# Three output-gate blocks of a hyena, attention and expert layer are computed between the first blocks of the hyena's projection instead of beside the attention

## The chip, the cores and the metric

One core of a Trainium2 chip runs the whole program. The metric is the device time of one execution in microseconds (us). The kernel before was run three times: 1930.4, 1916.2 and 1919.15 us, median 1919.15 us.

## What is computed

The reference is one transformer-like layer for 512 tokens of width 1024. The part that matters here is the token mixer:

```
z = h @ w_in + b_in
q, k, v = z[..., COL_Q:COL_K], z[..., COL_K:COL_V], z[..., COL_V:COL_G_HY]
y_hy = hyena(z[..., COL_HY:COL_Q]) @ w_hy_out
y_na = attend(q, k, v) @ w_na_out
gate = sigmoid(z[..., COL_G_HY:N_PROJ])
merged = gate[..., :D_MODEL] * y_hy + gate[..., D_MODEL:] * y_na
return merged @ w_out
```

`z` has 40 column blocks of 128: 12 for the hyena (blocks 0 to 3 are its value, 4 to 11 its two gates), 12 for the attention's q, k and v, and 16 for the output gates (blocks 24 to 39). The hyena convolves with long filters by Fourier transforms; the attention works on a window of the token grid and on 256 context tokens. A layer of sparse experts follows and takes the larger part of the time; the change does not touch it.

## The kernel before, in words

TensorE (PE) does all products, with 32-bit floats that are split into a high and a low half: a weight block is fetched into a tile `raw`, ScalarE (ACT) rounds it to `wh` (line 206), VectorE (DVE) subtracts to get `wl` (line 207). `raw` has three buffers, `wh` and `wl` two each, and all the stages share them. A column block of `z` is one call of `z_col` (line 469): `weights` fetches and splits, `project` (line 229) issues 16 matmuls of 512 columns with `wh` (line 235) and 8 with `wl` (line 237), and the sum stands in one of the two PSUM tiles called `a`. ACT then drains that tile with the bias added: into `zpad` for a hyena block (line 489 in `hy_block`), into `gz` or `t` for an output gate (line 591 in `gate`). `gate` stores its block to DRAM (line 592, queue SP); the merge at the end of the mixer loads all 16 again (`gl`, line 924).

The stages around the change, in the order of time:

- Filters and the hyena's first blocks (`run`, lines 850 to 862). The loop over `cb` computes blocks 0 to 3 of `z` and, after each, one step of the second filter (`drain(f1, 1)`). Behind block 1 it loads the context, computes its norm (`rstd`: sums of squares, transposes on line 405, a reduction on 407, a square root on 408, a reciprocal on 409, transposes back on 412) and its modulated form `hc`.
- The hyena (`hyena`, line 543): transposes of `y` (505), spectra (`spectrum`, 225 to 227 into tiles `s`, sums on DVE in 330 to 334), products with the filters (513 to 523), inverse transforms, and the eight gate blocks of the hyena. Beside it the modulation vector 2 is built from eight blocks of `w_ada` (`late_module`: ACT in 447 and 451, GpSimd additions in 452), and six output gates are computed at the steps in `HG`, the first of them at step 1.
- The attention (lines 876 to 909): 16 units, four blocks of queries for each of four pairs of heads. Step n issues the scores of unit n (`attn_scores`), the transposes of unit n-1 (`attn_turn`), one step of the projection for the next pair of heads, then `GATES[n]` items of the list `fill`, then the product with v of unit n-2 (`attn_out`, 749 and 750) and the store of unit n-3 (759). `fill` holds what is left of the output gates, then the eight blocks of the hyena's output product (`hy_out`, 12 matmuls each). What is left after step 16 is issued at step 17, with `issue_after(turn)`.
- The merge (`gated`, `out_proj`).

The order written here is not the final one: a scheduler in the compiler moves instructions on each engine by its own estimate, within what the data allow. Each engine then works through its own list in that order.

Of the kernel before, what the change touches and what calls it, by code (L numbers as in the profile page):

```python
# [153 lines left out]

GATES = [2, 1, 0, 1, 0, 1, 0, 1, 1, 1, 0, 1, 2, 2, 1, 2, 1]

LA = (0, 2)

# [11 lines left out]
class Kernel:  # L172
# [613 lines left out]
    def run(self, st):  # L786
# [17 lines left out]
        def drain(g, n=None):  # L804
            while n is None or n > 0:
                try:
                    next(g)
                except StopIteration:
                    return False
                n = None if n is None else n - 1  # L810
            return True

        dst = ExitStack()
        with ExitStack() as s1:
            dft = self.t(self.pool(dst, "dft", side="right"), "dft", [128, 2, 2, 4, 256], F32R)
            fp = self.pool(s1, "filt", side="right")
            cst = ExitStack()
            with ExitStack() as s0:
                xp = self.pool(s0, "x", side="left")
                cc = self.load(k, "cc")  # L820
                self.silu = k.tile([128, 8, 2], F32, name="silu_c")
                nc.scalar.activation(self.silu, cc, AF.Silu)
                mlp = self.filter_mlp(fp)
                cond = self.conditioning(xp)
                drain(mlp, 1)
                xT = self.load(xp, "xT")
                steps = [next(cond) for _ in range(2)]
                self.ident = self.load(k, "ident")
                for n, t in (("bada", "b_ada"), ("ng", "norm_g"), ("bin", "b_in"), ("cw", "cw"), ("skip", "skip")):
                    setattr(self, n, self.load(k, t))  # L830
                drain(mlp, 1)
                steps += [next(cond) for _ in range(2)]
                drain(mlp)
                r = self.rstd(xp, xT, 4)
                with self.tc.issue_after(self.squared):
                    nc.gpsimd.dma_start(dft, self.A["dft"])
                steps += [next(cond) for _ in range(2)]
                f0 = self.filters(0, fp, dft, steps[F4AT])
                drain(f0, 1)
                steps += list(cond)  # L840
                self.hold = steps[-1]
                self.modulate(xp, self.h, xT, self.a1[:, :, 0], self.sh1[:, :, 0], r)
            hst2 = ExitStack()
            vp = self.pool(hst2, "hyv", side="left")
            y = [self.t(vp, "yv", [128, 512], bufs=4) for _ in range(4)]
            cp = self.pool(cst, "hctx", side="left")
            self.hc = [self.t(cp, f"hc{x}", [128, 8, 256], F32R) for x in range(2)]
            zst = ExitStack()
            zp = self.pool(zst, "hyz", side="left")
            f1 = self.filters(1, fp, dft, self.hold)  # L850
            drain(f0)
            drain(f1, 1)
            for cb in range(4):
                self.hy_block(cb, y[cb], zp)
                if cb == 1:
                    xc = self.load(zp, "ctxT")
                    rc = self.rstd(zp, xc, 2)
                    self.modulate(zp, self.hc, xc, self.a1[:, :, 1], self.sh1[:, :, 1], rc, bufs=4)
                drain(f1, 1)
            pending = list(range(16))  # L860
            drain(f1)
            zst.close()
        yst = ExitStack()
# [12 lines left out]
        with ExitStack() as s1:  # L876
# [13 lines left out]
            for n in range(len(units) + 3):  # L890
# [12 lines left out]
                with self.tc.issue_after(turn) if n >= 17 else ExitStack():  # L903
                    for _ in range(min(GATES[n], len(fill)) if n < 17 else len(fill)):
                        fill.pop(0)()
# [398 lines left out]
```

## Time and profile before

| | |
|---|---|
| median of three runs | 1919.15 us |
| the profiled execution | 1923.32 us, span 1921.6 us, granted PE clock 0.98 |
| PE busy | 1817.9 us (95%) |
| DVE busy | 1507.1 us (78%) |
| ACT busy | 851.1 us (44%) |
| GpSimd busy | 583.1 us (30%) |

Times in the views below are us from the start of the span. A group's row gives a line, an engine, an operation, the tiles written and read, and how many. A row of the timeline gives start, duration, engine, line and, in brackets, the idle time of the engine ahead of it with what ended it. A row by stretch gives for each engine its busy time with the number of instructions, the granted PE clock as a share of 2.4 GHz, the share of the DMA engines and GB/s.

### The profile page before, as it was taken

What the parts mean: (1) busy time and instruction counts of PE and PEld (TensorE: products, weight loads), DVE (VectorE), ACT (ScalarE), POOL (GpSimd) and SP (SyncE); (2) the same over time, 40 slices, a digit from 0 to 9 for tenths busy, and PEclk for the clock granted to TensorE, in tenths of its full rate; (3) what the DMA queues carried; (4) which work ended last, traced back from release to release, by engine and by line L of the source; (5) the groups of instructions that cost most, each with busy time, mean ns of one, the idle gap of its engine ahead of it and who ended that gap; (6) DMA issues with size and microseconds to landing.
All of it is one profiled execution on the core that took longest, in us unless ns stands there. A gap on an engine that the chain in (4) does not pass through costs nothing.

```text
span 1921.6 us, 26565 instructions
## 1 busy us (share of the span) xinstructions
PE 1817.9 (95%) x9747; PEld 1566.6 (82%) x9747; DVE 1507.1 (78%) x2755; ACT 851.1 (44%) x1271; POOL 583.1 (30%) x363
## 2 busy tenths in 40 slices
PE   6999999999999988889999999999999999999987
PEld 1577887888877777789988898899999999987875
DVE  7869874556578699998997867887777777778876
ACT  2554334555563533336876333333333333333342
POOL 3443000000002533331221444444444444433431
PEclk9989999999999999999999999999999999999999
DMA  8445323322277322236988988989998888778874
GB/s 302 139 145 174 121 91 97 94 85 79 79 267 243 99 75 72 76 129 237 329 311 308 352 300 306 334 312 323 328 324 297 317 317 308 279 272 305 296 264 130
DMA packets 166843, 428.29 MB, mean 223 GB/s; under 512 B 14679, under 2 KB 70167, under 8 KB 162744
## 3 DMA queue, kind: packets, MB, share of 16 engines
q1 hardware_dynamic: 129128, 288.16, 44.5%
q0 software_dynamic: 37584, 138.43, 19.4%
q8 instruction: 76, 1.25, 0.3%
q14 instruction: 55, 0.45, 0.1%
HBM read 386.69 MB, written 37.75 MB: 221 GB/s over the span
## 4 chain that ended last, share of the span: by engine, by line
PE 62%; DVE 18%; issue 6%; DMA 5%; POOL 3%; ACT 2%; SPq 0%; ACTq 0%; DVEq 0%; POOLq 0%
PE a L235 24%; PE a L237 11%; PE s L225 5%; PE s L226 5%; PE s L227 5%; POOL row L1272 3%; PE t L225 2%; PE t L227 2%; PE t L226 2%; DVE f L1193 2%; PE s L1258 1%; PE s L1259 1%; DMA row<-in_u_rows,ei 1%; DVE vl L207 1%; DVE h2n L1286 1%
## 5 line engine op out<-in xcount | busy, mean ns | idle before, releaser
L235 PE MATMUL a<-h,wh 128*128 128x384 f32 (+1 forms) x2944 | 617.2, 359 | 9.8 <-ACT ring L1015 5.2
L235 PEld LDWEIGHTS a<-h,wh 128*128 128x128 f32 x2944 | 528.1, 191 | 58.2 <-ACT ring L1015 5.5
L206 ACT ACTIVATE wh<-raw 128x1024 fp32r<-128x1024 f32 (+1 forms) x208 | 213.6, 1027 | 370.5 <-DMA raw<-in_u_cols 156.3
L237 PE MATMUL a<-h,wl 128*128 128x384 f32 (+1 forms) x1472 | 317.0, 354 | 0.0
L1272 POOL DMA_INDIRECT row<-in_u_rows,ei x128 | 184.7, 1443 | 335.4 <-DVE row L1277 319.6
L1272 POOL DMA_INDIRECT row<-in_v_rows,ei x128 | 198.2, 1549 | 272.5 <-DVE h2n L1286 259.1
L237 PEld LDWEIGHTS a<-h,wl 128*128 128x128 f32 x1472 | 262.8, 189 | 17.6
L207 DVE TENSOR_TENSOR wl<-raw,wh 128x1024 fp32r<-128x1024 f32 (+1 forms) x173 | 202.9, 1173 | 52.2 <-ACT wh L206 30.8
L226 PE MATMUL s<-vl,wsh 128*128 128x512 f32 x512 | 201.3, 393 | 9.8 <-DVE vl L207 9.8
L227 PE MATMUL s<-vh,wsl 128*128 128x512 f32 x512 | 198.8, 390 | 0.0
L1277 DVE SCALAR_TENSOR_TENSOR row<-row,h2n 128x1024 f32<-128x1024 f32 x128 | 155.2, 1221 | 51.4 <-DMA row<-in_u_rows,ei 51.2
L206 ACT ACTIVATE wsh<-w 128x384 fp32r<-128x384 f32 x128 | 66.9, 523 | 277.5 <-PE t L226 145.8
L225 PE MATMUL s<-vh,wsh 128*128 128x512 f32 x512 | 176.4, 391 | 3.7 <-ACT vh L206 2.2
L1286 DVE SCALAR_TENSOR_TENSOR h2n<-row,dots,h2n 128x1024 f32<-128x1024 f32 x127 | 162.5, 1280 | 17.9 <-DMA row<-in_v_rows,ei 17.7
L397 POOL TENSOR_TENSOR sqs<-sqs,sq 128x512 f32<-128x512 f32 (+1 forms) x20 | 31.5, 1576 | 430.7 <-ACT sq L396 430.0
L207 DVE TENSOR_TENSOR vl<-raw,vh 128x1024 fp32r<-128x1024 f32 x128 | 155.9, 1218 | 7.7 <-ACT vh L206 7.7
L207 DVE TENSOR_TENSOR wsl<-w,wsh 128x384 fp32r<-128x384 f32 x128 | 78.1, 610 | 97.4 <-ACT wsh L206 97.3
L206 ACT ACTIVATE vh<-raw 128x1024 fp32r<-128x1024 f32 x128 | 134.4, 1050 | 22.1 <-DMA raw<-in_v_rows 21.6
L207 POOL TENSOR_TENSOR wl<-raw,wh 128x1024 fp32r<-128x1024 f32 x35 | 87.0, 2486 | 129.1 <-PE a L237 116.3
L226 PEld LDWEIGHTS s<-vl,wsh 128*128 128x128 f32 x512 | 96.3, 188 | 31.0 <-DVE vl L207 13.8
L225 PEld LDWEIGHTS s<-vh,wsh 128*128 128x128 f32 x512 | 95.9, 188 | 22.6 <-ACT vh L206 3.9
L227 PEld LDWEIGHTS s<-vh,wsl 128*128 128x128 f32 x512 | 96.4, 188 | 20.0 <-issue 0.2
(357 smaller groups left out, 3030.6 us busy)
## 6 DMA issues: line engine op xcount, KB each, us to landing
raw<-in_u_cols SPq DMA_DIRECT2D x128, 512.0 KB, 4.2
raw<-in_v_rows SPq DMA_DIRECT2D x128, 512.0 KB, 4.2
Gd<-st SPq DMA_DIRECT2D x24, 1024.0 KB, 5.2
G<-Gd SPq DMA_DIRECT2D x16, 1536.0 KB, 11.1
raw<-in_w_in SPq DMA_DIRECT2D x40, 512.0 KB, 3.5
adaw<-in_w_ada SPq DMA_DIRECT2D x16, 512.0 KB, 4.6
raw<-in_w_q SPq DMA_DIRECT2D x16, 512.0 KB, 3.4
wada<-in_w_ada SPq DMA_DIRECT2D x8, 512.0 KB, 8.9
```

What stands on the lines that cost most here:

```text
L206: return (nc.scalar.activation(hi, src, AF.Copy).ins, (nc.vector if eng == "v" else nc.gpsimd).tensor_tensor(lo, src, hi, ALU.subtract).ins)
L207: (nc.vector if eng == "v" else nc.gpsimd).tensor_tensor(lo, src, hi, ALU.subtract).ins)
L225: t.matmul(out, a[0], b[0], start=start, stop=False)
L226: t.matmul(out, a[0], b[1], start=False, stop=False)
L227: return t.matmul(out, a[1], b[0], start=False, stop=stop).ins
L235: t.matmul(out, w[0][:, c, :], h[x][:, c, :], start=(c == 0 and x == 0), stop=False)
L237: i = t.matmul(out, w[1][:, c, :], h[0][:, c, :], start=False, stop=(c == n - 1))
L397: self.squared = (nc.vector if db in dve else nc.gpsimd).tensor_tensor(acc, acc, sq, ALU.add).ins
L1193: V.tensor_tensor(m, mv[:, :, 0, :], mv[:, :, 1, :], ALU.add)
L1272: nc.gpsimd.indirect_dma_start(out=r, out_offset=None, in_=self.A[tab], in_offset=bass.IndirectOffsetOnAxis(ap=ei[:, n:n + 1], axis=0))
L1277: V.scalar_tensor_tensor(r, r, 1.0, h2n, op0=ALU.mult, op1=ALU.mult, accum_out=dots[:, n:n + 1])
L1286: V.scalar_tensor_tensor(acc, r, dots[:, n:n + 1], acc, op0=ALU.mult, op1=ALU.add)
```

## The change

The list of pending gates is made ahead of the loop over the hyena's first blocks, and after blocks 1, 2 and 3 one gate is computed (output gates 0, 1 and 2), with its `gz` in the pool of that stage. Thirteen gates remain: six beside the hyena as before, and seven in `fill` where there were ten. `GATES` has 15 items now where it had 17, so that with the list of 15 nothing is left over for step 17.

```
-GATES = [2, 1, 0, 1, 0, 1, 0, 1, 1, 1, 0, 1, 2, 2, 1, 2, 1]
+GATES = [1, 1, 0, 1, 0, 1, 0, 1, 1, 0, 1, 1, 1, 2, 1, 2, 1]
...
             drain(f0)
             drain(f1, 1)
+            pending = list(range(16))
             for cb in range(4):
                 self.hy_block(cb, y[cb], zp)
...
                 drain(f1, 1)
-            pending = list(range(16))
+                if cb:
+                    self.gate(pending.pop(0), zp)
             drain(f1)
```

The list of PE behind the context's norm, before: `a_874` and `a_946` are the hyena's blocks 2 and 3, `a_1103` is the output gate of step 1 of the hyena, `s_1039` its first spectrum. Each block has 16 rows of line 235 and one of line 237.

```order
L412 MATMUL a_805<-ident_144,rs_801 128x128 x2
L235 MATMUL a_874<-h_80,wh_870 128x512
...
L237 MATMUL a_874<-h_80,wl_871 128x512 x8
...
L237 MATMUL a_946<-h_80,wl_943 128x512 x8
...
L237 MATMUL a_1103<-h_80,wl_1100 128x512 x8
L225 MATMUL s_1039<-yth_1010,dft_85 128x256
```

The same place after the change: `a_874` is output gate 0, `a_908` the hyena's block 2, `a_980` gate 1, `a_1014` block 3, `a_1070` gate 2, `a_1205` the gate of step 1.

```order
L412 MATMUL a_805<-ident_144,rs_801 128x128 x2
L235 MATMUL a_874<-h_80,wh_870 128x512
...
L237 MATMUL a_874<-h_80,wl_871 128x512 x8
...
L237 MATMUL a_908<-h_80,wl_905 128x512 x8
...
L237 MATMUL a_980<-h_80,wl_977 128x512 x8
...
L237 MATMUL a_1014<-h_80,wl_1011 128x512 x8
...
L237 MATMUL a_1070<-h_80,wl_1067 128x512 x8
...
L237 MATMUL a_1205<-h_80,wl_1202 128x512 x8
L225 MATMUL s_1141<-yth_1112,dft_85 128x256
```

All three added blocks stand in one row of six, behind the transposes of the context's norm (line 412) and ahead of the hyena's first spectrum.

ACT beside these blocks, before: it drains block 2 (`zpad_899`), block 3 (`zpad_971`) and the gate (`gz_1128`); `raw_1186` is a block of `w_ada`.

```order
L489 ACTIVATE zpad_899<-a_874,b_in_150 128x4x8x16
L206 ACTIVATE hc_107_446<-md_835 128x256
L431 ACTIVATE md_845<-md_845,mod_368,a_393 128x256
L206 ACTIVATE hc_107_446<-md_845 128x256
L206 ACTIVATE hc_107_446<-md_840 128x256
L451 ACTIVATE raw_1186<-raw_1186,silu_c 128x1024
L489 ACTIVATE zpad_971<-a_946,b_in_150 128x4x8x16
L206 ACTIVATE yth_1010<-t_1007 128x256
L206 ACTIVATE yth_1017<-t_1014 128x256
L447 ACTIVATE adaacc_1003<-raw_1035,silu_c 128x1024
L591 ACTIVATE gz_1128<-a_1103,b_in_150 128x512
```

After the change, from the drain of block 2 to the first `yth`: `wh_1201` is the high half of the weights for the sixth block, `raw_1195` and `raw_1288` are blocks of `w_ada`.

```order
L489 ACTIVATE zpad_933<-a_908,b_in_150 128x4x8x16
L206 ACTIVATE wh_1066<-raw_1064 128x1024
L451 ACTIVATE raw_1195<-raw_1195,silu_c 128x1024
L591 ACTIVATE gz_1005<-a_980,b_in_150 128x512
L206 ACTIVATE wh_1201<-raw_1199 128x1024
L489 ACTIVATE zpad_1039<-a_1014,b_in_150 128x4x8x16
L451 ACTIVATE raw_1288<-raw_1288,silu_c 128x1024
L591 ACTIVATE gz_1095<-a_1070,b_in_150 128x512
L206 ACTIVATE yth_1112<-t_1109 128x256
L206 ACTIVATE yth_1119<-t_1116 128x256
```

The drains of three blocks now stand right behind instructions that read a freshly fetched tile `raw`.

The list of PE at the end of the attention, before: the last transposes (line 733) of unit 15, a block of `hy_out` (`a_5259`), then the product with v of unit 15.

```order
L750 MATMUL a_5231<-vv_4031,pcl_5101 128x64
L733 MATMUL t_5197<-ident_144,s_5079 128x128 x2
L733 MATMUL t_5204<-ident_144,s_5086 128x128 x2
L235 MATMUL a_5259<-y_546_2627,wh_5262 128x512
...
L237 MATMUL a_5259<-y_546_2627,wl_5263 128x512 x4
L749 MATMUL a_5279<-vv_4031,pl_1147_5200 128x128
```

After the change:

```order
L750 MATMUL a_5251<-vv_4099,pcl_5121 128x64
L733 MATMUL t_5217<-ident_144,s_5099 128x128 x2
L733 MATMUL t_5224<-ident_144,s_5106 128x128 x2
L749 MATMUL a_5279<-vv_4099,pl_1151_5220 128x128
L759 MATMUL t_5275<-ident_144,o_1145_5201 128x128
L750 MATMUL a_5279<-vv_4099,pl_1152_5221 128x64
```

No block stands between the last transposes and the product that reads them; all eight blocks of `hy_out` stand further ahead.

## Rows read from the trace of the kernel before

**Rows 1.** Busy time by stretch: first blocks, early hyena, late hyena, attention.

```profile
120.00:141.40 21.40, 19.32 (x80) 15.43 (x79) 15.12 (x36) 12.64 (x23) 5.95 (x9) 0.92 0.67 221
141.40:180.00 38.60, 33.92 (x188) 29.31 (x187) 35.38 (x53) 17.80 (x28) 14.59 (x6) 0.91 0.59 205
180.00:283.00 103.00, 103.00 (x593) 89.89 (x592) 83.87 (x150) 36.99 (x53) 3.73 (x1) 1.00 0.34 110
283.00:541.00 258.00, 254.07 (x1519) 212.10 (x1518) 148.68 (x368) 139.68 (x317) 0.00 (x0) 0.99 0.28 84
```

**Rows 2.** What PE waited for from 85 to 180: us in total, times, longest.

```profile
PE s L225 <- DVE X L332: 4.0, 1, 4.0
PE s L225 <- DVE K L332: 2.5, 1, 2.5
PE a L412 <- DVE rs L409: 2.1, 1, 2.1
```

**Rows 3.** Timeline of PE: the three blocks behind the context's norm.

```profile
122.92 5.52 PE L235 MATMUL a<-h,wh 128*128 128x512 f32 x16
...
130.14 3.89 PE L235 MATMUL a<-h,wh 128*128 128x512 f32 x16
133.88 2.03 PE L237 MATMUL a<-h,wl 128*128 128x512 f32 x8
135.74 3.89 PE L235 MATMUL a<-h,wh 128*128 128x512 f32 x16
...
141.34 0.28 PE L225 MATMUL s<-yth,dft 128*128 128x256 f32 x1
```

**Rows 4.** Timelines of DVE and ACT: the context's norm.

```profile
119.29 0.42 DVE L407 TENSOR_REDUCE rs<-t 128x2 f32<-128x256 f32 x1 [0.57 <-PE t L405]
...
120.89 1.28 ACT L408 ACT_TABLE_LOAD   x1
...
122.51 0.17 DVE L409 RECIPROCAL rs<-rs 128x2 f32<-128x2 f32 x1 [0.32 <-ACT rs L408]
```

**Rows 5.** Timeline of DVE: one operation beside a GpSimd addition, the next without.

```profile
168.51 2.58 DVE L520 TENSOR_TENSOR X<-Ya 128x256 f32<-128x256 f32 x1
171.01 0.41 DVE L521 TENSOR_TENSOR X<-Ya 128x256 f32<-128x256 f32 x1
```

**Rows 6.** Costliest groups: the low half of a weight block on DVE.

```profile
L207 DVE TENSOR_TENSOR wl<-raw,wh 128x1024 fp32r<-128x1024 f32 (+1 forms) x173 | 202.9, 1173 | 52.2 <-ACT wh L206 30.8
```

**Rows 7.** What PE waited for from 283 to 541, the attention.

```profile
PE a L235 <- ACT t L604: 1.8, 2, 1.4
...
PE t L733 <- DVE pcl L207: 0.5, 2, 0.3
```

**Rows 8.** Timelines of PE and DVE: the end of the attention.

```profile
535.24 0.44 PE L733 MATMUL t<-ident,s 128*128 128x128 f32 x2 [0.27 <-DVE pcl L207]
535.43 2.09 PE L235 MATMUL a<-y,wh 128*128 128x512 f32 x8
...
536.13 0.43 DVE L207 TENSOR_TENSOR pl<-t,pl 128x256 fp32r<-128x256 f32 x1
```

**Rows 9.** Timelines of PE and ACT: last scores, last exponentials, first transposes of unit 15.

```profile
521.03 0.27 PE L227 MATMUL s<-kT,qT 64*128 64x256 f32 x1
...
526.84 0.53 ACT L713 ACTIVATE s<-s,mx 128x256 f32<-128x256 f32 x1
...
533.14 0.62 PE L727 MATMUL t<-ident,ec 128*128 128x128 f32 x4
```

**Rows 10.** Timeline of ACT: a block of `w_ada` and the drain behind it.

```profile
135.60 1.15 ACT L451 ACTIVATE raw<-raw,silu_c 128x1024 f32<-128x1024 f32 x1 [2.83 <-DMA raw<-in_w_ada]
136.66 0.70 ACT L489 ACTIVATE zpad<-a,b_in 128x512 f32<-128x512 f32 x1
```

**Rows 11.** DMA issues: tiles, queue, count, KB each, median us from issue to landing.

```profile
raw<-in_w_in SPq DMA_DIRECT2D x40, 512.0 KB, 3.5
...
wh<-in_w_ada SPq DMA_DIRECT2D x4, 512.0 KB, 12.6
```

More of the change, by code (lines that the diff above doesn't have):

```diff
@@ L153, in layout @@
     return {k: np.ascontiguousarray(v, dtype=np.float32) for k, v in a.items()}
-GATES = [2, 1, 0, 1, 0, 1, 0, 1, 1, 1, 0, 1, 2, 2, 1, 2, 1]
+GATES = [1, 1, 0, 1, 0, 1, 0, 1, 1, 0, 1, 1, 1, 2, 1, 2, 1]
 LA = (0, 2)
@@ L852, in run @@
             drain(f1, 1)
+            pending = list(range(16))
             for cb in range(4):
@@ L859, in run @@
                 drain(f1, 1)
-            pending = list(range(16))
+                if cb:
+                    self.gate(pending.pop(0), zp)
             drain(f1)
```

## The prediction

> **What bounds the kernel now.** I read the busy time by stretch first, because the change takes work out of one stage and puts it into another, and only the limits of these two matter. In the attention, where three gates leave, PE is busy 254.07 of 258 us and DVE 148.68 [rows 1]: PE is the bound, and a block less is its whole duration less. In the first blocks of the hyena, where three gates arrive, PE is busy 19.32 of 21.40 us and DVE 15.12; in the early part of the hyena behind it DVE has 35.38 of 38.60 and PE 33.92; in the late part PE has 103.00 of 103.00 [rows 1]. So room for free PE work exists only in the early hyena, some 4.7 us of it, and a little ahead of the first blocks.
>
> Next come the waits of PE from 85 to 180: one of 4.0 us and one of 2.5 us in the spectra (line 332), and one of 2.1 us on the reciprocal of the context's norm (line 409) [rows 2]. A moved gate gains only where it is issued into one of these. Then the order: all three gates stand in one row of six blocks, behind the transposes of the context's norm and ahead of the first spectrum. The waits of 2.1 and 2.5 us lie ahead of that row, the one of 4.0 us behind it. None of the three is filled by a gate.
>
> Last come the timelines, for the duration of a block and for the chains at the edges.
>
> **The change part by part.** Each sum is made against the profiled execution, 1923.32 us, which lies 4.2 us above the median of 1919.15; I take the difference over to the median unchanged.
>
> *Three blocks added in the hyena's first blocks.* One block is 16 matmuls of line 235 and 8 of line 237. From one block's start to the next it takes 135.74 − 130.14 = 5.60 us, and 141.34 − 135.74 = 5.60 again [rows 3]. The first block of the row takes 130.14 − 122.92 = 7.22, since its 16 matmuls last 5.52 us and not 3.89 [rows 3]; there is one first block before and after, so this is not paid again. Three more: 3 × 5.60 = +16.8 us. Each brings one rounding on ACT and one subtraction on DVE of 1.17 us [rows 6]: 3 × 1.17 = 3.5 us of DVE beside 16.8 us of PE, which DVE had room for (15.12 of 21.40). No part of the 16.8 lies beside a stall, so all of it counts.
>
> *Three blocks taken out of the attention.* The same 24 matmuls and the same operands' sizes: −16.8 us, if PE stays the bound. It does by the rows: only 3.9 us of 258 are without matmuls, and the waits that the profile shows there reach 1.4 us at most [rows 7]. The remaining fillers lie between units whose chains get less cover. For that I add 0.6 us (0 to 8; the upper end is worked out under rival C).
>
> *The context's norm.* In the new order the transposes of line 405 stand two matmuls earlier, the reduction of line 407 stands ahead of a hyena operation on DVE, and the load of the square root's table on ACT (1.28 us, line 408) stands ahead of a copy. The reduction began at 119.29 and the reciprocal at 122.51 [rows 4], and PE waited 2.1 us for it [rows 2]. What the chain passes is two matmuls of 0.28 [rows 3], one DVE operation of 0.41 [rows 5] and one copy that I put at the same 0.4: an estimate of 1.4 to 1.5 us. So the wait falls to some 0.6: −1.5 us. The bounds are 0 (the chain is only late elsewhere) and −3.3: the whole wait, and the slower start of the row behind it, 5.52 − 3.89 = 1.6 us with the shorter pause ahead of it, of which I count 1.2.
>
> *The end of the attention.* Before, a block of `hy_out` covers the way from the last transposes to the product with v: the transposes of line 733 start at 535.24 and last 0.44, and DVE's split, which the product reads, starts at 536.13 and lasts 0.43, so it ends at 536.56 [rows 8]. Now nothing stands between, and PE stalls from 535.68 to 536.56, at most 0.9 us; the split can come earlier when nothing else delays DVE. I take +0.4. The upper end is 2 us, about that block's own 2.09 of line 235 [rows 8], if the exposed store and the merge slip too. The softmax of the last unit does not come into it: its last scores end at 521.30, its last exponential at 527.37, and its first transposes start at 533.14 [rows 9], so that 5.8 us of cover are left, as much as one full block.
>
> *The additions of GpSimd.* The modulation vector's additions (line 452) stretch a DVE operation beside them from 0.41 to 2.58 us, that is by 2.2 [rows 5]. Their order on GpSimd is unchanged; I count 0, with −2.2 (one falls into the longer row of blocks, where DVE has room) and +4.4 (two more fall into the part where DVE is the bound).
>
> *ACT's list.* Drains of the longer row now stand behind instructions that read fresh tiles. Before, the operation of line 451 on such a tile waited 2.83 us for its transfer and began at 135.60, and the drain of block 3 behind it began only at 136.66 [rows 10]. After, three drains and the rounding `wh_1201` stand so. A plain weight block lands 3.5 us after issue, but four tiles of `w_ada` took 12.6 [rows 11]. I count 0, for the list starts 16.8 us ahead of the spectra and the transfers get that time as well; 6 us is the upper end, below.
>
> The Trainium skill, page "PSUM — Partial Sum Buffer", section "Engine vs sequencer instructions", says that "ScalarE/VectorE/GpSimdE queues are strict FIFO" and that matmuls start in program order. It speaks against this change: a drain whose sum is ready still waits behind the late transfer ahead of it, and by it alone the term would be +6, not 0. The drain at 136.66, right behind the operation that had waited 2.83 us, agrees [rows 10].
>
> Sum: +16.8 − 16.8 + 0.6 − 1.5 + 0.4 + 0 + 0 = −0.5 us: 1922.8 in terms of the profiled execution, 1918.6 in terms of the median. With the bounds that can go together, the forecast's own range is 1914 (−2.2 and the rest of −3.3) to 1925 (+4.4 and the tail's 1.6 more).
>
> **The rivals.** *B, the gates fill PE's idle time.* If the chip runs the row so that the spectra find their inputs ready, because DVE works ahead during the longer row, the 4.0 us wait goes, with the 2.1 of the norm, and the slow start of 1.6: −7.7, 1911. For it: the early hyena has 38.60 − 33.92 = 4.7 us without matmuls [rows 1]. Against it: DVE is the bound there with 35.38 of 38.60, the operations that it is late with need the spectra that come after the row, and no gate moved behind that wait. Chance 0.11.
>
> *C, the attention loses its cover; slower.* In the last pair of heads the projections are over, and between the scores and the transposes of a unit PE has only what `GATES` gives it. The chain of a unit takes 527.37 − 521.30 = 6.1 us [rows 9]. One block of 5.60 us, or one of `hy_out`, is less than this; with the product and the transposes of the neighbours it is about the same. Where PE's work between falls below 6.1 us, it waits. Steps 9 and 12 lose one item each and the tail shifts: if six units each wait as long as the longest wait shown, 1.4 us [rows 7], that is 8.4 us, 1927. For it: waits on ACT (lines 604 and 643) are already there. Against it: 5.8 us spare in the last unit [rows 9], and step 10 gains one. Chance 0.13.
>
> *D, a drain behind a late transfer.* The two tiles `a` are refilled in turn, so a block cannot start before the drain of the one two earlier. If the transfer ahead of such a drain lands 12.6 us after issue and not 3.5 [rows 11], it is 9.1 us late; one block, 5.60, is still ahead of PE, so it stalls 3.5 us, and the weights of the sixth block (`wh_1201`), which stand behind, slip with it by up to 2.5 more: +6, 1924.6. For it: the 2.83 us before [rows 10]. Against it: that wait held up no matmul (none of [rows 2] lies in the row). Chance 0.06.
>
> *E, the change does not do what it says*, because the blocks are moved back by the compiler: the order shows them moved, so this has no chance of its own.
>
> **How the numbers follow.** The forecast, 1918.6, has the remaining 0.70. A measurement of this kernel tells about 1% from no change, 19.2 us, as the three runs from 1916.2 to 1930.4 suggest. All cases above lie within 8.5 us of the median. To be faster by over 1% the change would have to hide all 16.8 us and something more, for which PE has no idle time: 0.02. Slower by over 1% wants C and D at their worst, with the tail, 8.4 + 6 + 2 + 4.4 = 20.8: 0.04. The range, 1910 to 1929, reaches from B's 1911 to C's 1927 with 1 to 2 us for the spread of a median of three.
>
> **What would show it.** Right: six blocks of line 235 and 237 without a gap, about 7.2 + 5 × 5.60 = 35.2 us from the norm's transposes to the first spectrum; the wait of line 412 on DVE below 1 us; the 4.0 us wait of the spectra still there, 3 to 5; the attention shorter by 16 to 17 us with PE busy in over 97% of it; at its end a wait of the product (line 749) on DVE's split of 0.4 to 0.9. Wrong: if the wait on X (line 332) has gone, B holds; if waits of lines 727 to 750 on ACT or DVE in the attention add up to over 6 us, C; if PE waits in the row of six on drains (lines 489, 591) or on `wh`, D. If the time differs by more than 10 us and none of these rows has changed, the difference comes from the later stages, which I took as untouched.

## The result and the profile after

The changed kernel takes 1937.51 us (median of nine runs, 1928.31 to 1942.32), the kernel before in nine runs 1919.37 (1911.34 to 1930.40): ratio 1.0072, 95% interval 1.0050 to 1.0094. The two medians lie 18.1 us apart; the ratio, by which all kernels are compared below, puts the loss at 13.8 us, within 9.6 to 18. That is less than 1% and yet clear of zero. The forecast was no change, 1918.6, and the range ended at 1929.

The profiled execution of the changed kernel took 1931.2 us, span 1929.4. By stretch (time from:to, length, then for each engine the busy time and the instructions, the granted clock, the DMA share, GB/s): the row of six blocks, the early hyena, the late hyena, the attention. They answer to [rows 1].

```profile
117.00:151.10 34.10, 33.90 (x147) 27.29 (x148) 17.52 (x38) 16.60 (x28) 3.56 (x5) 1.00 0.48 149
151.10:188.10 37.00, 32.09 (x189) 27.32 (x187) 33.80 (x51) 16.66 (x27) 17.16 (x10) 1.00 0.76 264
188.10:289.00 100.90, 100.88 (x574) 87.77 (x575) 85.00 (x151) 37.18 (x53) 3.74 (x1) 1.00 0.35 114
289.00:546.40 257.40, 247.87 (x1467) 207.51 (x1465) 145.29 (x365) 136.17 (x312) 0.00 (x0) 0.97 0.24 74
```

Three blocks have left the attention, and it is as long as it was: 257.40 us where it had 258.00. PE is idle there for 9.5 us, before for 3.9, and the granted clock is 0.97 instead of 0.99. From the first transposes of a norm (line 622) to the last store's transpose (line 759) the same is seen more sharply, for between these two points the traces hold the same matmuls of lines 235 and 237 but for the 48 and 24 of the three blocks; first before, then after:

```profile
302.63:541.59 238.96, 236.45 (x1413) 196.75 (x1412) 139.61 (x353) 129.41 (x300) 0.00 (x0) 0.99 0.29 85
```

```profile
310.62:546.34 235.72, 227.60 (x1342) 189.75 (x1340) 135.41 (x350) 125.08 (x294) 0.00 (x0) 0.96 0.25 75
```

The three blocks are 16.8 us. Without them 238.96 should have become 222.2; it became 235.72. So 13.6 us came back in: 5.6 as idle time of PE, 8.0 as busy time, fewer matmuls and each of them longer on average. (The two profiled executions lie only 7.8 us apart in their spans, +8.0 ahead of this stretch, −3.2 in it and +3.1 behind it; the rest of the difference between the medians is not in these two traces.)

Where it came in is told by the waits of PE in the attention after the change (us in total, times, longest):

```profile
PE a L749 <- ACT t L643: 2.9, 2, 2.2
...
PE t L647 <- DVE t L623: 1.6, 1, 1.6
```

Before, the first was a single wait of 0.4 us and the second did not appear; the longest in [rows 7], 1.4, stands ahead of the attention's first scores in both. The timeline of PE (start, duration, operation, in brackets the wait and what ended it) shows the first of the two places. The units are counted from 0. The scores of units 0 to 3 are done, and ahead of unit 4 the projection of the next pair of heads does its norm: line 622 transposes the scale of q to be multiplied in, line 647 transposes v. The same comes again ahead of units 8 and 12.

```profile
355.95 3.98 PE L235 MATMUL a<-h,wh 128*128 128x512 f32 x16
...
361.95 0.60 PE L622 MATMUL t<-ident,t 128*128 128x128 f32 x4
364.17 0.66 PE L647 MATMUL t<-ident,t 128*128 128x128 f32 x4 [1.61 <-DVE t L623]
364.72 0.63 PE L622 MATMUL t<-ident,t 128*128 128x128 f32 x4
366.14 0.46 PE L749 MATMUL a<-vv,pl 128*128 128x128 f32 x1 [0.79 <-ACT t L643]
...
372.33 5.83 PE L235 MATMUL a<-h,wh 128*128 128x512 f32 x16 [0.26 <-ACT t L591]
```

The same place in the kernel before:

```profile
354.80 0.65 PE L622 MATMUL t<-ident,t 128*128 128x128 f32 x4
355.21 3.97 PE L235 MATMUL a<-h,wh 128*128 128x512 f32 x16
359.02 0.63 PE L237 MATMUL a<-h,wl 128*128 128x512 f32 x2
359.48 0.60 PE L647 MATMUL t<-ident,t 128*128 128x128 f32 x4
...
361.08 0.60 PE L622 MATMUL t<-ident,t 128*128 128x128 f32 x4
```

Before, an output gate's block stood between lines 622 and 647, and PE had work while DVE multiplied (line 623) and gave the PSUM tile `t` free. After, the same block stands ahead of line 622, at 355.95, and nothing stands between: PE waits 1.61 us for the tile `t`, then 0.79 for the tile `a` that ACT drains in line 643. Behind the wait 16 matmuls of line 235 take 5.83 us, not 3.97.

The second place is unit 12. There it is the wait for `a` alone, behind line 647; first before, where a block stands behind that line (and score products ahead of it), then after, where nothing does:

```profile
473.87 0.66 PE L647 MATMUL t<-ident,t 128*128 128x128 f32 x4
474.28 3.50 PE L235 MATMUL a<-h,wh 128*128 128x512 f32 x14
```

```profile
482.17 0.66 PE L647 MATMUL t<-ident,t 128*128 128x128 f32 x4
484.98 0.33 PE L749 MATMUL a<-vv,pl 128*128 128x128 f32 x1 [2.15 <-ACT t L643]
```

By stretch after the change, the wait and what follows it, at unit 4 and at unit 12:

```profile
361.90:366.20 4.30, 1.90 (x15) 1.31 (x13) 4.21 (x9) 2.54 (x7) 0.00 (x0) 1.00 0.42 144
366.20:376.70 10.50, 10.24 (x38) 8.97 (x39) 4.92 (x11) 2.86 (x7) 0.00 (x0) 0.51 0.31 93
481.40:485.10 3.70, 1.41 (x9) 0.94 (x10) 3.01 (x9) 3.36 (x8) 0.00 (x0) 1.00 0.60 179
485.10:492.70 7.60, 7.60 (x31) 6.78 (x32) 4.22 (x11) 3.24 (x10) 0.00 (x0) 0.55 0.24 68
```

At each place PE is idle for 2.3 to 2.4 us at a granted clock of 1.00, that is 2.4 GHz, and then works for 10.50 and 7.60 us at 0.51 and 0.55, about 1.2 GHz. At half the clock that gives away 10.50 × 0.49 + 7.60 × 0.45 = 8.6 us, which with the idle 4.7 makes 13.3. The kernel before has a slow stretch of its own in the attention, which the changed kernel lacks:

```profile
506.00:510.00 4.00, 4.00 (x13) 3.24 (x13) 1.10 (x5) 2.06 (x9) 0.00 (x0) 0.57 0.29 85
```

It gave away 4.00 × 0.43 = 1.7 us. So by this estimate the two places account for 11.6 of the 13.6 us.

At unit 8 the kernel before has only two matmuls of line 237 between lines 622 and 647, and PE waits 0.4 us there (line 749) with no slow stretch behind it. So not every thin place costs; why this one does not was not tried.

### The profile page after: what moved, and what is told of

Read it like the earlier page. It is cut to its first block, busy times and chain, and to the rows that moved or that the text cites. A ratio compares the mean times of both kernels' runs of the same rounds, so it can differ in the third digit from the quotient of the medians.

```text
span 1929.4 us, 26579 instructions
## 1 busy us (share of the span) xinstructions
PE 1823.3 (94%) x9747; PEld 1572.2 (81%) x9747; DVE 1505.1 (78%) x2755; ACT 852.8 (44%) x1271; POOL 586.3 (30%) x363
## 4 chain that ended last, share of the span: by engine, by line
PE 66%; DVE 18%; DMA 4%; issue 3%; ACT 2%; POOL 1%; SPq 0%; ACTq 0%; DVEq 0%; POOLq 0%
PE a L235 25%; PE a L237 12%; PE s L225 6%; PE s L226 6%; PE s L227 6%; PE t L226 2%; PE t L227 2%; PE t L225 2%; DVE f L1195 1%; DMA row<-in_u_rows,ei 1%; PE s L1260 1%; POOL row L1274 1%; PE s L1261 1%; DVE gh L1254 1%; PE a L749 1%
## 5 line engine op out<-in xcount | busy, mean ns | idle before, releaser
L226 PEld LDWEIGHTS s<-vl,wsh 128*128 128x128 f32 x512 | 96.7, 189 | 30.8 <-DVE vl L207 13.6
```

The costliest lines, as they stand in the source:

```text
L226: t.matmul(out, a[0], b[1], start=False, stop=False)
```

## The experiments

The ratios below are to runs of the kernel before on the same chip, with 95% intervals. Theory 1 is the one just read from the trace; theory 2 puts the loss to the blocks that arrive beside the hyena, theory 3 to the number of items in the attention as a whole, rival C of the prediction.

| kernel | bare places (nothing between lines 622 and 647) | ratio, interval |
|---|---|---|
| the change | units 4 and 12 | 1.0072 (1.0050 to 1.0094) |
| item of step 10 to step 0 | none | 1.0014 (0.9994 to 1.0034) |
| item of step 10 to step 9 | unit 4 | 1.0037 (1.0017 to 1.0057) |
| item of step 8 to step 0 | unit 12 | 1.0075 (1.0048 to 1.0102) |
| item of step 5 to step 0 | units 8 and 12 | 1.0092 (1.0066 to 1.0118) |
| the new table alone, no gate moved | units 4 and 12 | 1.0098 (1.0074 to 1.0121) |
| three blocks added, none taken away | none | 1.0056 (1.0034 to 1.0077) |
| the change, bare places filled with junk | unit 8 (4 and 12 hold the junk) | 1.0020 (1.0003 to 1.0037) |
| two gates moved | none | 1.0000 (0.9981 to 1.0019) |
| one gate, behind block 1 | none | 1.0020 (1.0002 to 1.0038) |
| one gate, behind block 3 | none | 1.0007 (0.9987 to 1.0026) |
| one gate into the early hyena, step 2 | none | 0.9987 (0.9968 to 1.0006) |
| one gate into the early hyena, step 4 | none | 0.9986 (0.9966 to 1.0007) |

**The table mended at step 0.** With seven gates left only seven items may stand in steps 0 to 10, since a block of `hy_out` needs the tiles `yo` made at step 11. So an item is moved, not added.

```diff
-GATES = [1, 1, 0, 1, 0, 1, 0, 1, 1, 0, 1, 1, 1, 2, 1, 2, 1]
+GATES = [2, 1, 0, 1, 0, 1, 0, 1, 1, 0, 0, 1, 1, 2, 1, 2, 1]
```

Expected: 

> The changed kernel with one item of GATES put back to step 0 (taken from step 10): the order of the attention's first eight steps is that of the kernel before again, with a gate block between the transposes of lines 622 and 647 at unit 4, and a block of hy_out there at unit 12. Theory 1 (lost cover: at these two places PE had nothing between the two lines, stood 2 to 3 us for DVE and ACT, and then ran 7 to 11 us at 1.2 GHz): the waits of lines 647 and 749 on ACT and DVE fall below 1 us, the granted clock of the attention is back at 0.99, and the time is 14 to 16 us below that of the changed kernel, 1918 to 1924. Theory 2 (the blocks added beside the hyena cost the time, the slow stretches of the attention are chance): 1934 to 1940, as the changed kernel. Theory 3 (rival C of the prediction, too few items in the whole attention): no gain either, since step 10 loses what step 0 gets.

Measured: 1925.91 us, ratio 1.0014: 0.0058 or 11 us less than the change, somewhat short of the 14 to 16 expected, but four fifths of the loss, by one item of the table. The attention, between the same two points:

```profile
311.82:538.02 226.20, 220.51 (x1341) 183.24 (x1340) 135.25 (x350) 123.72 (x294) 0.00 (x0) 1.00 0.27 78
```

It is 9.5 us shorter than that of the changed kernel with the same work: 2.4 us less idle, 7.1 less busy, at a clock of 1.00 and not 0.96. That is still 4.0 us above the 222.2 that three blocks less should give. Line 749's wait on line 643 is back at 0.4. Theory 2 and theory 3 both expected no gain.

**The table mended at step 9 alone.**

```diff
-GATES = [1, 1, 0, 1, 0, 1, 0, 1, 1, 0, 1, 1, 1, 2, 1, 2, 1]
+GATES = [1, 1, 0, 1, 0, 1, 0, 1, 1, 1, 0, 1, 1, 2, 1, 2, 1]
```

Expected: 

> The changed kernel with the item of step 10 put back to step 9, as before the change. The order has a block of hy_out between lines 622 and 647 at unit 12, and still nothing between them at unit 4. Theory 1: only the second slow stretch (about 485 us) goes, the first (about 362 us) stays: 5 to 8 us below the changed kernel, about 1931. Theory 2: 1934 to 1940. Theory 3: 1934 to 1940.

Measured: 1930.94, ratio 1.0037. One place is mended, half of the loss is gone, though the interval still touches that of the change. By stretch, what follows unit 4, still bare, and the time around unit 12, now with a block there:

```profile
366.00:380.00 14.00, 10.82 (x48) 8.80 (x47) 6.37 (x13) 4.39 (x11) 0.00 (x0) 0.63 0.36 114
475.00:500.00 25.00, 23.54 (x160) 20.63 (x158) 14.67 (x35) 14.52 (x33) 0.00 (x0) 1.00 0.21 58
```

**The new table without the moved gates.** This is the kernel before with the one line of `GATES` exchanged.

```diff
-GATES = [2, 1, 0, 1, 0, 1, 0, 1, 1, 1, 0, 1, 2, 2, 1, 2, 1]
+GATES = [1, 1, 0, 1, 0, 1, 0, 1, 1, 0, 1, 1, 1, 2, 1, 2, 1]
```

Expected: 

> The kernel before with only the table GATES of the changed kernel: no gate beside the hyena's first blocks, ten gates and eight blocks of hy_out beside the attention, three items of them left for step 17. The order has nothing between lines 622 and 647 at units 4 and 12. Theory 1: the two waits and slow stretches appear here too; the work is that of the kernel before, so 1919 + 15 = 1934, within 6. Theory 2: no loss, 1919 within 5.

Measured: 1941.94, ratio 1.0098, 19 us slower, though no work was added and nothing beside the hyena was touched. The two places, wait and what follows:

```profile
349.00:358.20 9.20, 4.71 (x39) 3.89 (x37) 5.95 (x14) 4.48 (x12) 0.00 (x0) 0.97 0.40 128
358.20:361.00 2.80, 2.80 (x7) 2.22 (x8) 2.77 (x7) 0.94 (x2) 0.00 (x0) 0.50 0.27 97
470.00:474.40 4.40, 1.39 (x10) 0.84 (x8) 3.19 (x11) 4.20 (x12) 0.00 (x0) 0.92 0.40 115
474.40:483.50 9.10, 8.62 (x31) 7.75 (x32) 4.42 (x9) 2.74 (x7) 0.00 (x0) 0.50 0.18 52
```

This contradicts theory 2. It lost 19 and not the 15 expected; the interval, 14 to 23, holds both, and no run tells apart whether the three items left over for step 17 cost something; in the trace PE is busy for 70.02 of the last 70.69 us of the attention, at a clock of 1.00, so no wait and no slow stretch stands there. The change has the same table and ratio 1.0072: with the table the same, the three moved gates make the time some 5 us less and not more, which the intervals do not set apart from nothing.

**Three blocks added.** Gates 0 to 2 are computed beside the hyena's first blocks and once more in the attention, so the text of this kernel does 16.8 us more than is needed.

```diff
                 drain(f1, 1)
+                if cb:
+                    self.gate(cb - 1, zp)
             pending = list(range(16))
```

Expected: 

> The kernel before with three blocks more: output gates 0, 1 and 2 are computed a second time, beside the hyena's first blocks, and the attention keeps its table and its ten gates. This prices the side where the blocks arrive. Theory 1: the blocks cost what they last or somewhat less, 16.8 less the 3 to 10 us by which the spectra and the norm gain: 1926 to 1936, with the attention as before. Theory 2: the side of the hyena costs more than the blocks themselves, 16.8 + 15, about 1950.

Measured: 1932.63, ratio 1.0056 or 10.8 us (6.5 to 14.8). So the arrival of three blocks costs less than they last, as theory 1 had it, and theory 2's 1950 is far off. The attention is that of the kernel before (238.96 us), between the same two points:

```profile
311.70:549.98 238.28, 235.18 (x1414) 195.62 (x1412) 139.82 (x353) 129.23 (x300) 0.00 (x0) 1.00 0.29 86
```

**One gate, and two.** With one gate moved the old table has exactly its 17 items; with two, step 12 loses one.

```diff
-                if cb:
+                if cb == 1:
                     self.gate(pending.pop(0), zp)
```

Expected, behind block 1: 

> One gate only is moved, behind the hyena's block 1, and GATES is the table of the kernel before, whose 17 items the 9 gates and 8 blocks of hy_out just fill; at units 4 and 12 the order has blocks between lines 622 and 647 as before. Theory 1 (lost cover was the loss): what the block costs beside the hyena is less than its 5.60 us, since the norm's wait and the slow start behind it shrink with the first block already, and the attention gives the whole 5.6 back: ratio 0.996 to 1.000 to the kernel before. Rival (the attention gives nothing for a block that leaves, wherever it leaves): 1.001 to 1.003.

Expected, behind block 3: 

> As the run before, with the one gate behind block 3. If the gain beside the hyena is the earlier chain of the norm (lines 405 to 409), brought forward by a gate issued right behind it, this kernel gains less than the one with the gate behind block 1, by 1 to 4 us; if it is the longer row of PE work ahead of the spectra, in which DVE works ahead, both gain the same.

Expected, two, behind blocks 1 and 3: 

> Two gates are moved, behind blocks 1 and 3; GATES is that of the kernel before with one item less at step 12. The places at units 4 and 12 are covered (unit 12 by a block of hy_out). Theory 1: ratio 0.996 to 1.001, between the kernel with one gate and the one with three and a mended table (1.0014). Rival: 1.003 to 1.005.

Measured: 1.0020, 1.0007 and 1.0000. The two single gates do not differ beyond their intervals, so the question behind them, the norm's chain or the longer row, stays open. The first lies above what theory 1 gave (0.996 to 1.000), where the rival had it (1.001 to 1.003), by an interval that just leaves 1.000 out; the second and its interval reach both; two gates came out as theory 1 had it, and not at the rival's 1.003 to 1.005. Together they say: where the places stay covered, moving gates costs little (ratios of 1.0000 to 1.0020) and gains nothing that can be measured.

**The bare places filled with junk.**

```diff
         self.qk_norm(0, tq, r[:, 0:4], qT, ap)
+        if j in (1, 3):
+            with self.tc.issue_after(self.turn):
+                junk = self.ps("s")
+                for n in range(16):
+                    nc.tensor.transpose(junk[:, n % 4 * 128:n % 4 * 128 + 128], self.ident, self.ident)
```

Expected: 

> The changed kernel with 32 transposes of the identity added whose result nobody reads, 16 behind the transposes of line 622 at each of units 4 and 12 (the scheduler also moves some score products there). They do no work that is wanted and cost PE about 0.11 us each, 3.6 us in all. If half of the loss there is the 1.2 GHz that follows the wait, PE stays at 2.4 GHz in both places and the time falls below that of the changed kernel (ratio 1.0072) by 4 to 9 us, to 1.003 to 1.005, though work was added. If only the waiting itself costs, it stays at 1.007 or goes up to 1.009.

Measured: 1926.25, ratio 1.0020, 10 us faster than the change by adding work to it, and a little more than the 4 to 9 expected. Unit 4 (the junk is line 676, and lines behind it are shifted by five):

```profile
361.12 0.60 PE L622 MATMUL t<-ident,t 128*128 128x128 f32 x4
361.56 1.91 PE L676 MATMUL s<-ident 128*128 128x128 f32 x16
363.40 0.38 PE L225 MATMUL s<-kT,qT 64*128 64x256 f32 x1
...
364.65 0.60 PE L647 MATMUL t<-ident,t 128*128 128x128 f32 x4
```

```profile
361.12:368.60 7.48, 7.42 (x64) 6.66 (x62) 6.22 (x14) 3.84 (x8) 0.00 (x0) 1.00 0.14 32
```

PE is idle there for 0.06 of 7.48 us and stays at 1.00. Line 647 starts 3.53 us behind line 622, in the changed kernel only 2.22: the wait itself was not shortened, it was filled. What went is the 1.2 GHz behind it. Nine score products moved in as well, so the 10 us are not the junk's alone. One other slow stretch stood in this trace, and it has the same cause: unit 8, where no junk was put, has lost its block to a place ahead of line 622, and is bare in this kernel (lines 754 and 643 are 749 and 643 of the others):

```profile
422.82 0.60 PE L647 MATMUL t<-ident,t 128*128 128x128 f32 x4
424.48 0.33 PE L754 MATMUL a<-vv,pl 128*128 128x128 f32 x1 [1.05 <-ACT t L643]
```

```profile
426.00:433.00 7.00, 6.43 (x25) 5.45 (x24) 3.95 (x8) 1.86 (x4) 0.00 (x0) 0.51 0.31 93
```

The gain speaks for the clock, and not the waiting alone, as the larger part: in the changed kernel PE is idle for 4.7 us at the two places together, and no filling could win more than that without the clock. But the two intervals put the gain anywhere from 4.7 to 15 us, so that its lower end does not rule out the waiting alone.

**The bare place elsewhere.**

```diff
-GATES = [1, 1, 0, 1, 0, 1, 0, 1, 1, 0, 1, 1, 1, 2, 1, 2, 1]
+GATES = [2, 1, 0, 1, 0, 1, 0, 1, 0, 0, 1, 1, 1, 2, 1, 2, 1]
```

Expected: 

> The changed kernel with one item of GATES moved from step 8 to step 0: unit 4 has its block between lines 622 and 647 again, unit 12 has none, the opposite of the run with the item at step 9. Theory 1 (each bare place costs about 5 us by its wait and the 1.2 GHz behind it): one bare place, so between the mended table (1.0014) and the changed kernel (1.0072), 1.003 to 1.006, with one slow stretch in the attention at unit 12. Rival (what counts is how many items lie in the first eight steps): as the mended table, 1.000 to 1.003.

Measured: 1.0075, above the 1.003 to 1.006 of theory 1, which its interval still reaches, and clear of the rival's upper end. Unit 12 has its stretch, 489 to 493; but a second one stood at 459 to 466, where no norm is and PE had been busy without a gap for the 19 us ahead of it, and that one has no cause here:

```profile
485.00:489.20 4.20, 1.91 (x16) 1.56 (x15) 2.68 (x7) 4.19 (x11) 0.00 (x0) 1.00 0.54 166
489.20:493.00 3.80, 3.80 (x18) 3.41 (x18) 2.83 (x8) 1.05 (x5) 0.00 (x0) 0.56 0.20 43
459.00:466.00 7.00, 7.00 (x20) 4.91 (x20) 1.66 (x6) 0.88 (x3) 0.00 (x0) 0.51 0.15 45
```

So the loss does not simply add up by places. The other kernel of this pair has step 5's item at step 0 (`[2, 1, 0, 1, 0, 0, 0, 1, 1, 0, 1, ...]`).

Expected: 

> The changed kernel with one item moved from step 5 to step 0: unit 4 is covered, and units 8 and 12 have nothing between lines 622 and 647. Theory 1: two bare places again, at another unit: 1.005 to 1.009, as the changed kernel, and waits of lines 647 and 749 with a slow stretch at units 8 and 12. Rival (unit 4 alone is special, or the early steps): 1.000 to 1.004.

Measured: 1.0092, at the upper end of theory 1. Unit 8, which is covered in the change, is now slow, and unit 4 is not:

```profile
425.00:428.80 3.80, 0.97 (x8) 0.52 (x5) 3.37 (x7) 3.77 (x12) 0.00 (x0) 0.93 0.61 160
428.80:438.50 9.70, 9.27 (x34) 8.35 (x35) 4.73 (x9) 2.79 (x7) 0.00 (x0) 0.50 0.31 94
489.00:493.00 4.00, 1.16 (x11) 0.92 (x9) 1.97 (x5) 3.61 (x12) 0.00 (x0) 1.00 0.45 128
493.00:499.60 6.60, 6.60 (x25) 5.81 (x25) 3.62 (x7) 1.27 (x4) 0.00 (x0) 0.51 0.19 59
```

The loss goes where the bare place goes. It is not a matter of unit 4 or of the early steps.

**A gate where PE does wait.** Two kernels put one gate of the attention into the early hyena, with the table of before:

```diff
-HG = (1, 3, 15, 16, 17, 18)
+HG = (1, 2, 3, 15, 16, 17, 18)
```

Expected, step 2: 

> The kernel before with one gate moved from the attention into the early hyena (HG gets step 2), where DVE is the bound: the order has one block more ahead of the spectrum for which PE waited 4.0 us for DVE (line 332) and behind which it ran some 7 us at 1.2 GHz. Theory 1, that a block costs nothing where it stands in a wait that would send the clock down: the block's 5.60 us go into the 4.0 and the 3.5 lost behind it, the attention gives 5.6 back: ratio 0.995 to 0.999. Rival (DVE is the bound there, and the block's own subtraction of 1.17 us and its order push DVE later): 1.000 to 1.003.

Expected, step 4: 

> As the run before, with the gate at step 4, one spectrum later in the order. Theory 1: 0.995 to 0.999, less if the block now stands behind the wait instead of in it (then 1.000). Rival: 1.000 to 1.003.

Measured: 0.9987 and 0.9986. Each interval reaches into the forecast of theory 1 and holds no change, the rival's lower end, too. The wait on X (line 332), 4.0 us in [rows 2], is gone in both. What is left in the first, from 118 to 200 us:

```profile
PE a L412 <- DVE rs L409: 2.1, 1, 2.1
PE t L505 <- DVE mod L387: 1.7, 1, 1.7
PE t L505 <- DVE ytl L207: 0.5, 1, 0.5
```

If there is a kernel better than both in this family it is one of these, by some 2.5 us, which the runs don't establish.

## Why the prediction was wrong

**The three blocks added, +16.8.** Right as a term: the row has its six blocks without a gap, now from 117.39 to 151.08, 33.7 us or six times 5.6, the first one at full speed. So the row became 15.3 us longer than the 18.4 of its three blocks before, and not 16.8: the slow start of 1.6, which the sum took as paid before and after alike, was gone.

**The norm, −1.5, and the early hyena.** Right in direction, too small: the waits after the change from 85 to 189 us include

```profile
PE a L237 <- DVE wl L207: 2.5, 1, 2.5
...
PE s L225 <- DVE K L332: 1.5, 1, 1.5
...
PE a L412 <- DVE rs L409: 0.6, 1, 0.6
```

The norm's wait fell to 0.6 as predicted. The 4.0 us on X, which I said would stay, went, and why it went stays open; others on `wl` and `wh` came, so that PE is idle as long as before (37.00 − 32.09 = 4.9 us), but in shorter pieces, and the clock of this stage is 1.00 where [rows 1] had 0.91. By the prediction's own sign, the wait on X, this is rival B, to which I gave 0.11. The run with three added blocks puts this whole side at +10.8 (6.5 to 14.8): not the +15.3 of the forecast, which the interval just leaves out, and near B's 16.8 − 7.7 = 9.1.

**The three blocks taken out, −16.8, "if PE stays the bound. It does by the rows".** This is the step that failed. The whole result, +13.8, less the arrival, +10.8, leaves +3.0 where −16.8 was put: some 20 us, with intervals of about 4 on each. The reason given, that PE is busy 254.07 of 258 us, shows only that all of PE's work is needed, not that the order of it can be thinned: PE is that busy because work stands in the places where a chain through DVE and ACT must be waited out. With a mended table (1.0014 against 1.0056) the departure is worth −8.1; in the profiles of these two kernels the attention falls from 238.28 to 226.20, by 12.1. So even with the places covered it was not seen to give back the whole 16.8, and where the rest stays is open.

**The +0.6 for other boundaries, 0 to 8.** This term was to hold the loss, and it measured 13.6 in the trace, where the attention became 3.2 us shorter and not the 16 to 17 of the prediction's signs. Rival C had the kind of mechanism right, lost cover, and put it in the wrong place (the softmax of the last pair of heads, six units at 1.4 us) and at the wrong price; its sign, waits of over 6 us on lines 727 to 750, did not come either, for these add up to 3.3 us, and what the clock took shows in no wait. The place is the norm of q and k with the transposes of v, once for each pair of heads; the price is 2.3 us of wait and about twice that for the clock. Rival C also says that steps 9 and 12 lose one item each and passes over step 0, which loses one too; put back there (and taken from step 10), one item covered both places and took four fifths of the loss away. Place and price could have been read: the list of PE has no block between lines 622 and 647 at units 4 and 12 after the change, and [rows 2, 3] showed that behind a wait of 2.1 us 16 matmuls last 5.52 us and not 3.89. I used that price for the norm of the context and not for any wait in the attention.

The Trainium skill, page "TensorE: Matmul & The Clock Gate", section "HAM oscillation — how this bites in real kernels", describes a kernel in which PE waits so long between groups of matmuls that each next group starts at the lower clock, and advises an order of the work that keeps it busy. The trace agrees in that the lower clock follows a wait: 2.4 us idle at unit 4, then 10.50 us at 0.51. In the page's case it is one wait for a DMA, here two short ones for DVE and ACT.

**The tail, +0.4.** Too high if anything: no wait there is longer than 0.3 us, and line 749 has none. **ACT's list, 0, and rival D.** Right: no matmul of the six-block row waited for a drain. **GpSimd's additions, 0.** Not seen apart.

## What to carry to other kernels

A filler block is worth its place, not its length: before one is taken out of a stage whose PE is 98% busy, look in the new order of PE for two neighbours that depend on each other through DVE or ACT with nothing between them. Price such a place by the wait and by what the clock takes behind it, from a row where the same kernel already waits; here the second part was about twice the first. And a table that sets the order is an edit of its own: the new one cost 1% by itself, with no block moved out of the attention. Cover put into one place can come out of another: the junk kernel filled units 4 and 12 and bared unit 8.

## What the runs showed that was not expected

Useless work made the kernel faster: 32 transposes of the identity, 3.8 us of PE, took the ratio from 1.0072 to 1.0020.

A wait need not be in one piece. At unit 4 the longest single wait was 1.61 us and PE was busy for 1.90 of 4.30 us, and the clock still fell to 0.51 for 10.50 us without a further gap above 0.3. And some slow stretches came where no wait of this kind stands (459 to 466 us in one kernel, 506 to 510 in the kernel before, at clocks of 0.51 and 0.57): their cause was not tried, and they may be part of the spread of one kernel's runs (19 us for the kernel before).
